# Merge weights finished in one step, four merge operations moved ahead, and the low weight parts last in each product

## The chip, the cores and the metric

The kernel runs on one core of a Trainium2 chip. The core has a matrix engine (TensorE, PE in the profile, with weight loads listed as PEld), a vector engine (DVE), a scalar engine (ACT), GpSimd (POOL), and a queue (SP) from which this kernel issues all of its transfers between HBM and the core's own memory (SBUF). Matrix products land in the accumulators (PSUM). The metric is the device time of one execution in microseconds; less is better.

## The reference

Two layers over a sequence of 1024 rows of 1024 values. Layer 0 is dilated sliding-window attention, gated; layer 1 is a state-space layer. The change lies in layer 0:

```python
proj = h @ w_in
qkv = proj[..., :n_qkv].reshape(B, S, 3, N_GROUPS_A, ATTN_HEADS, HEAD_DIM)
z = proj[..., n_qkv:]
outs, lses = [], []
for g, (window, dilation) in enumerate(DILATED_GROUPS):          # three groups
    o, l = dilated_group_attention(qkv[:, :, 0, g], qkv[:, :, 1, g], qkv[:, :, 2, g],
                                   rel_bias, window, dilation)
    outs.append(o)
    lses.append(l)
wts = jax.nn.softmax(jnp.stack(lses), axis=0)
o = jnp.sum(wts[..., None] * jnp.stack(outs).astype(jnp.float32), axis=0)
o = o.reshape(B, S, ATTN_WIDTH).astype(h.dtype)
return (o * jax.nn.silu(z)) @ w_out
```

So for each of 16 heads three attention outputs are computed, one for each group, and merged with weights that are a softmax over the three groups' log-sum-exps. The kernel calls these the merge's weights (the "group weights").

## The kernel before

The kernel first norms and transposes the input and computes all values v (up to about 334 us), then runs the attention (about 334 to 1050 us), then the gate, the output projection and layer 1. The attention works on *units*: unit m is the pair of heads p = m // 3 in group g = m mod 3, 24 units in all (class `Unit`).

Numbers are held in two parts. `split` (L100) makes a high part on ACT (L104) and a low part, the source minus the high part, on DVE or POOL (L105); a product then takes three matmuls instead of one: high x high, high x low, low x high.

The projection to queries and keys of one unit is done with seven products in place of eight (a Strassen scheme). `product(i)` (L560) accumulates twelve matmuls of 128 x 128 weights on 512 columns into bank X (i = 0, 5, 6, 3) or Y (i = 1, 4, 2); its operand is `w[:, y, ...]`, y = 0 the high and y = 1 the low part of the weights. `weights(i)` (L544) makes these two parts, the high one on ACT, the low one on POOL (tile wqk), and four such tiles exist at a time. `sums` and `qk` move the banks on and make q and k, with their low parts ql and kl on POOL (L105). `load` (L537) brings a unit's raw weights, two tiles of 512 KB (wraw), each as soon as the tile of the unit before is no longer read.

The rest of a unit's attention is spread over the two units that follow: `logits` (PE L665, DVE L671), `exps` (ACT L687), `T` (transposes on PE, L693, tile pt), `split_weights` (ACT and DVE, tile ph), `PV` (PE L742), `store` (ACT L761 and DVE L762). In the loop over m, `cur` is the unit whose projection runs, `one` the unit before, `two` the one before that, `nxt` the next one.

When the third group of a pair is done, its three outputs are merged, during the next two units. `put_ms` writes maxima and sums to HBM and `merge_load` reads them compactly; `merge_maxima` follows at the end of that unit. In the next unit, the one whose `two` has g = 0 and which is called a merging unit here, `merge_weights` (L810 to L813, four small operations on POOL) and `merge_store` (a reciprocal on DVE, L821, a multiplication on POOL, L822, and a write to HBM, wt_dr, L824) finish the weights. `merge` (L935) is a generator: each step of it issues one POOL operation. In the merging unit there are six: two multiplications of group 2's output by its weights and two of group 0's (L946), each with two loads of 128 KB (mw<-wt_dr, L945), and two additions (L949). Four buffers (ring tag b) hold the loaded weights. `more(n)` takes n steps of it. In other units `more` takes steps of `rotations` or of the merge's second part.

The order is written out by hand: `Program` (`step`, `run`) keeps the instructions of each step in this order on PE, ACT, DVE and POOL. SP's queue isn't bound by it; the planner that builds the program orders transfers by what is ready in its own simulated time and by priority, and the loads of raw weights have a raised priority. Each engine's queue, SP's too, is then worked off strictly in order on the chip.

Of the kernel before, what the change touches and what calls it, by code (L numbers as in the profile page):

```python
# [316 lines left out]
class Quads:  # L317
# [48 lines left out]
    done, jobs = 0, {}  # L366

    def quad(self, raw, order, product, banks, use):


# [144 lines left out]
class Unit:  # L515
# [44 lines left out]
    def product(self, i):  # L560
        c = self.c
        if i == 0:
            self.X = c.psx.tile([P, H], F32, tag="x", name="x")
        elif i in (1, 4):
            self.Y = c.psy.tile([P, H], F32, tag="y", name="y")
        ps = self.X if i in (0, 5, 6, 3) else self.Y
        w, rows = self.w.pop(i), c.forms[i]
        order = [(b, x, y) for b in range(4) for x, y in ((0, 0), (1, 0), (0, 1))]
        for m, (b, x, y) in enumerate(order):
            c.nc.tensor.matmul(ps, w[:, y, b * P:b * P + P], rows[x][:, b, :], start=i in (0, 1, 4) and m == 0,  # L570
                               stop=m == len(order) - 1, skip_group_check=True)
# [215 lines left out]
def merge_load(c, p):  # L787
    cm, e, d = c.compact
    src = bass.AP(c.ms_dr.tensor, c.ms_dr.offset + p * 3 * 4096, [[32, 64], [2048, 6], [1, 32]])
    c.nc.sync.dma_start(cm.rearrange("p g m n -> p (g m) n"), src)  # L790
# [66 lines left out]
def attn_units(c, w_in):  # L857

    nc, tc = c.nc, c.tc
    units = [Unit(c, m) for m in range(24)]  # L860
    c.outputs = [[] for _ in range(8)]
    step = Program(c)

    units[0].load(w_in)
    for i in (0, 1, 5):
        if i == 5:
            units[0].difference()
        units[0].weights(i)
    for m in range(26):
        cur = units[m] if m < 24 else None  # L870
        one = units[m - 1] if 1 <= m < 25 else None
        two = units[m - 2] if m >= 2 else None
        nxt = units[m + 1] if m + 1 < 24 else None

        def run(*steps):
            for unit, name, *args in steps:
                if unit is not None:
                    step(getattr(unit, name), *args)

        if one and one.g == 0:  # L880
            extra = rotations(c, one.p)
        elif two and c.merge is not None:
            extra = merge(c, c.merge, c.outputs[c.merge], two.g)
            if two.g == 1:
                c.merge = None
        else:
            extra = iter(())

        def more(n):
            for _ in range(n):  # L890
                step(next, extra, None)

        weigh = c.merge if two and two.g == 0 else None
        run((cur, "product", 0), (cur, "sums", 0), (two, "PV", 0, 1), (two, "T", 1, 0),
            (two, "split_weights", 1, 0), (two, "exps", 1, 1), (two, "store", 0, 1))
        if weigh is not None:
            step(merge_weights, c)
        run((cur, "weights", 6), (cur, "weights", 4))
        if weigh is None:
            more(1)  # L900
        run((cur, "product", 1), (cur, "sums", 1), (one, "logits", 0),
            (two, "PV", 1, 0), (two, "T", 1, 1), (two, "split_weights", 1, 1), (two, "store", 1, 0), (cur, "weights", 3))
        if weigh is not None:
            step(merge_store, c, weigh)
        else:
            more(2)
        run((cur, "product", 5), (cur, "sums", 5), (one, "logits", 1), (two, "PV", 1, 1))
        if two:
            c.pair = two.p
            step(put_ms, c, two.g, two.ms)  # L910
            if two.g == 2:
                merge_load(c, two.p)
        run((one, "split_v", 0), (one, "load_v", 1), (two, "store", 1, 1), (one, "exps", 0, 0), (cur, "weights", 2),
            (nxt, "load", w_in))
        more(5 if weigh is None else 2)
        run((cur, "product", 6), (cur, "sums", 6), (one, "logits", 2), (one, "exps", 0, 1), (cur, "product", 4),
            (cur, "sums", 4), (one, "T", 0, 0), (one, "split_weights", 0, 0), (one, "split_v", 1), (cur, "load_v", 0),
            (one, "logits", 3), (nxt, "difference"), (nxt, "weights", 0))
        if weigh is not None:
            more(4)  # L920
        run((cur, "qk", 1), (cur, "qk", 4),
            (cur, "product", 3), (cur, "qk", 3), (nxt, "weights", 1), (one, "PV", 0, 0), (one, "T", 0, 1),
            (one, "split_weights", 0, 1), (one, "exps", 1, 0), (cur, "product", 2), (cur, "sums", 2),
            (cur, "qk", 2), (one, "store", 0, 0))
        if two and two.g == 2 and two.p < 7:
            step(merge_maxima, c)
        run((nxt, "weights", 5))
        more(9)
        if two and two.g == 2:
            if two.p < 7:  # L930
                c.merge = two.p
            else:
                c.last = c.outputs[7]

def merge(c, p, O, part):  # L935


    nc = c.nc
    halves = [slice(n * H, n * H + H) for n in range(2)]
    for g in ((2, 0), (1,))[part]:  # L940
        for n, cols in enumerate(halves):
            w = c.slot("mw", tag="b")
            off = c.wt_dr.offset + (p * 3 + g) * 2048 + n * H
            for h in range(2):
                nc.sync.dma_start(w[HEADS[h]], bass.AP(c.wt_dr.tensor, off + h * S, [[0, 64], [1, H]]))  # L945
            nc.gpsimd.tensor_tensor(O[g][:, cols], O[g][:, cols], w, op=ALU.mult)  # L946
            yield
    for cols in halves:
        nc.gpsimd.tensor_tensor(O[2][:, cols], O[2][:, cols], O[part][:, cols], op=ALU.add)  # L949
        yield  # L950
    if part == 0:
        return
    if p >= EARLY:
        for cols in halves:
            w = c.slot("mg", tag="b")
            nc.sync.dma_start(w, c.g_dr[p, :, cols])
            nc.gpsimd.tensor_tensor(O[2][:, cols], O[2][:, cols], w, op=ALU.mult)
            yield
    nc.sync.dma_start(c.on_dr[p], O[2])
# [19 lines left out]
def attention(c, a):  # L979
# [60 lines left out]
    c.psa, c.psx, c.psy = c.ps("psa", 1), c.ps("psx", 1), c.ps("psy", 1)  # L1040
    c.attn = c.es_attn.enter_context(tc.tile_pool(name="attn", bufs=1, side="right", reuse_waits="tile"))
    attn_units(c, a["w_in"])
    return h

# [542 lines left out]
def rotations(c, et):  # L1587


    nc = c.nc  # L1590
    v = nc.gpsimd
    t = c.attn.tile([P, 192], F32, tag="rotc", name="rotc", bufs=1)
    for at, off, w in ((0, 0, 16), (128, S, 8)):
        src = bass.AP(c.tab_dr.tensor, c.tab_dr.offset + off + et * 4 * w, [[S + H, P], [32 * w, 2], [1, 4 * w]])
        nc.sync.dma_start(t[:, at:at + 8 * w].rearrange("p (n x) -> p n x", n=2), src)
    rot2 = [[t[:, at + n * 4 * w:at + (n + 1) * 4 * w].rearrange("p (k x) -> p k x", k=4) for n in range(2)]
            for at, w in ((0, 16), (128, 8))]
    shape = [P, 4, 8, 16]
    xr, xi = (y.unsqueeze(2).to_broadcast(shape) for y in rot2[0])
    wr, wi = (y.unsqueeze(3).to_broadcast(shape) for y in rot2[1])  # L1600

    def store(n, t):
        for s in range(2):
            dst = bass.AP(c.rot_dr.tensor, c.rot_dr.offset + (et * 3 + n) * 64 * S + s * P, [[S, 64], [256, 4], [1, P]])
            nc.sync.dma_start(dst, t[HEADS[s]].rearrange("p (k x) -> p k x", k=4))

    for part in range(2):
        out, tmp = c.slot("rt", tag="b"), c.slot("rtmp", tag="b")
        o, t = (x.rearrange("p (k j x) -> p k j x", k=4, j=8) for x in (out, tmp))
        v.tensor_tensor(o, xr, wi if part else wr, op=ALU.mult)  # L1610
        yield
        v.tensor_tensor(t, xi, wr if part else wi, op=ALU.mult)
        yield
        v.tensor_tensor(o, o, t, op=ALU.add if part else ALU.subtract)
        store(part, out)
        yield
    yield
    yield
    nc.scalar.activation(tmp, out, AF.Copy, scale=-1.0)
    store(2, tmp)  # L1620
# [381 lines left out]
```

## Time and profile before

| what | value |
|---|---|
| runs before | 1621.3, 1616.12, 1618.36 us; median 1618.36 |
| the profiled execution's own time | 1613.09 us |
| its span | 1610.9 us |
| PE, DVE, ACT, POOL busy | 98%, 65%, 50%, 43% of the span |
| granted TensorE clock | 0.997 |

The span is the time from the first to the last instruction in the profiled execution. Times in the profile's timeline are counted from its start. A timeline row gives the start, the duration, the engine, the line, the operation, the tile written and the tiles read, and the count of instructions in the row; in brackets stands the engine's idle time before it and what ended it.

### The profile page before, as it was taken

The page shows a single profiled execution, that of the slowest core. Times are in us where ns is not written, and L with a number is a line of the kernel's source. Part 1 is how long each engine was busy: PE and PEld are TensorE (multiplying, and loading weights), DVE is VectorE, ACT ScalarE, POOL GpSimd, SP SyncE. Part 2 cuts the span into 40 slices and gives each one's busy share as a digit, 9 for nine tenths or more (in the row PEclk, how much of TensorE's full clock was granted, in tenths as well). Part 3 has the DMA queues.
Part 4 walks back from the last instruction along what each step waited for, and adds up shares of the span by engine and source line. Part 5 has one row for each costly group of instructions (what it writes and reads, how often), then busy time and mean ns, then how long its engine had stood idle before and what let it go on. Part 6 is the DMA issues. An engine that isn't in the chain of part 4 may idle for free.

```text
span 1610.9 us, 26891 instructions
## 1 busy us (share of the span) xinstructions
PE 1578.2 (98%) x9462; PEld 1339.7 (83%) x9462; DVE 1053.9 (65%) x2532; ACT 806.2 (50%) x2004; POOL 699.0 (43%) x586
## 2 busy tenths in 40 slices
PE   8999999999999999999999999999999999999998
PEld 6889999988887888888888878887888888878886
DVE  8798889945555655655555656658563999855533
ACT  5232223337777677767677677754453223433411
POOL 1000001026577677686777777535220455522121
PEclk9999999999999999999999999999999999999999
DMA  6323444433223333414324333548347888565432
GB/s 257 118 54 111 155 145 147 150 116 89 70 70 106 101 90 102 111 60 110 103 70 125 95 103 101 129 146 234 104 157 204 247 246 258 171 190 175 157 118 79
DMA packets 185808, 216.43 MB, mean 134 GB/s; under 512 B 43060, under 2 KB 139079, under 8 KB 185161
## 3 DMA queue, kind: packets, MB, share of 16 engines
q1 hardware_dynamic: 185672, 214.72, 45.0%
q8 instruction: 74, 1.21, 0.3%
q14 instruction: 62, 0.50, 0.1%
HBM read 155.61 MB, written 59.06 MB: 133 GB/s over the span
## 4 chain that ended last, share of the span: by engine, by line
PE 61%; DVE 7%; POOL 6%; DMA 5%; issue 2%; SPq 2%; ACT 1%; DVEq 0%; POOLq 0%; ACTq 0%
PE x L570 14%; PE y L570 10%; PE pso L1178 10%; PE psj L130 8%; PE pso L742 5%; PE psq L449 4%; PE psl L665 4%; PE pt L693 3%; DMA mw<-wt_dr 2%; DVE T L1702 2%; PE psb L130 1%; DVE T L1707 1%; POOL O L946 1%; POOL O L949 1%; POOL wqk L105 1%
## 5 line engine op out<-in xcount | busy, mean ns | idle before, releaser
L105 POOL TENSOR_TENSOR wqk<-wraw,wqk 128x512 fp32r<-128x512 f32 x161 | 210.5, 1316 | 125.9 <-ACT wqk L104 119.1
L687 ACT ACTIVATE lg<-lg,nm 128x128 f32<-128x128 f32 (+1 forms) x384 | 168.6, 443 | 1.6
L105 DVE TENSOR_TENSOR ph<-pt,ph 128x512 fp32r<-128x512 f32 (+2 forms) x160 | 93.9, 620 | 99.0 <-ACT ph L104 98.9
L570 PE MATMUL x<-v,wqk 128*128 128x512 f32 x576 | 146.4, 403 | 0.7 <-ACT u L583 0.7
L570 PE MATMUL y<-v,wqk 128*128 128x512 f32 x576 | 145.4, 401 | 0.0
L671 DVE CUSTOM_DVE_ANT_0 lg<-psl,T 128x128 f32<-128x128 f32 (+1 forms) x384 | 110.6, 347 | 42.7 <-PE psl L665 41.6
L570 PE MATMUL x<-hh,wqk 128*128 128x512 f32 x384 | 130.4, 400 | 0.0
L1554 POOL TENSOR_TENSOR Ks<-Ks,O 128x16 f32<-128x16 f32 x8 | 4.1, 513 | 290.3 <-ACT Ks L1552 276.3
L570 PEld LDWEIGHTS y<-v,wqk 128*128 128x128 f32 x576 | 105.5, 188 | 23.7
L104 ACT CAST wqk<-wraw 128x512 fp32r<-128x512 f32 x168 | 102.5, 617 | 42.4 <-DVE wraw L550 24.5
L570 PEld LDWEIGHTS x<-v,wqk 128*128 128x128 f32 x576 | 104.5, 189 | 22.6 <-ACT u L583 1.1
L449 PE MATMUL psq<-whi,v 128*128 128x256 f32 x640 | 119.7, 284 | 0.0
L742 PEld LDWEIGHTS pso<-ph,vs 128*128 128x128 f32 x736 | 97.4, 189 | 9.8 <-DVE ph L105 0.8
L130 PE MATMUL psj<-h1h,whi 128*128 128x512 f32 (+1 forms) x272 | 103.4, 385 | 1.1 <-ACT h1h L104 1.1
L742 PE MATMUL pso<-ph,vs 128*128 128x256 f32 (+1 forms) x736 | 103.4, 281 | 0.2
L104 ACT CAST ph<-pt 128x512 fp32r<-128x512 f32 (+2 forms) x160 | 78.6, 533 | 48.1 <-PE pt L693 47.8
L130 PE MATMUL psj<-h1l,whi 128*128 128x512 f32 (+1 forms) x272 | 101.8, 379 | 0.2 <-DVE h1l L105 0.2
L449 PEld LDWEIGHTS psq<-whi,v 128*128 128x128 f32 x640 | 99.8, 189 | 1.2 <-ACT whi L104 0.6
L1205 POOL TENSOR_TENSOR xr<-xr,y 128x512 f32<-128x512 f32 x30 | 38.2, 1295 | 128.2 <-DVE y L1204 90.5
L104 ACT CAST whi<-v 128x1024 fp32r<-128x1024 f32 x35 | 36.7, 1050 | 108.4 <-PE psq L449 93.7
L449 PE MATMUL psq<-wlo,v 128*128 128x256 f32 x320 | 90.2, 283 | 0.0
L570 PEld LDWEIGHTS x<-hh,wqk 128*128 128x128 f32 x384 | 72.2, 188 | 17.6
(310 smaller groups left out, 4378.2 us busy)
## 6 DMA issues: line engine op xcount, KB each, us to landing
wraw<-in_w_in_dram SPq DMA_DIRECT2D x56, 512.0 KB
v<-in_w_v_dram SPq DMA_DIRECT2D x24, 512.0 KB
mw<-wt_dr SPq DMA_DIRECT2D x84, 128.0 KB
vp<-v_dr SPq DMA_DIRECT2D x32, 256.0 KB
wraw<-in_ssm_w_in_dram SPq DMA_DIRECT2D x16, 512.0 KB
v_dr<-v SPq DMA_DIRECT2D x30, 256.0 KB
ca_dr<-ca SPq DMA_DIRECT2D x32, 144.0 KB
CA<-ca_dr SPq DMA_DIRECT2D x8, 576.0 KB
```

The lines of the kernel that those rows point to most:

```text
L104: c.last_hi = nc.scalar.copy(hi, src).ins
L105: return (engine or nc.vector).tensor_tensor(lo, src, f32(hi), op=ALU.subtract)
L130: nc.tensor.matmul(ps, w[n == 2][:, k * P:k * P + P], h[n == 1][:, k, :], start=first and k == 0 and m == 0, stop=m == len(order) - 1 and ...
L449: nc.tensor.matmul(o, r[x][:, k, ts], w[y][:, k, :], skip_group_check=True, start=i in (0, 4, 5) and t % 2 == k == n == 0, stop=k == 3 and ...
L570: c.nc.tensor.matmul(ps, w[:, y, b * P:b * P + P], rows[x][:, b, :], start=i in (0, 1, 4) and m == 0, stop=m == len(order) - 1, skip_group ...
L665: nc.tensor.matmul(psl[:, h, o], x[HEADS[h], qs], y[HEADS[h], ks], start=j == js[0] and i == 0, stop=i == 2, skip_group_check=True)
L671: nc.vector.tensor_tensor_reduce(self.lg[u, j][:, h], psl[:, h, o], self.bt[:, h, 256 - w:256], scale=1.0, scalar=-3.0e38, op0=ALU.add, op ...
L687: c.nc.scalar.activation(t, t, AF.Exp, bias=self.nm[:, h, b:b + 1], accum_out=ms[:, col:col + 1])
L693: c.nc.tensor.transpose(pt[:, n * P:(n + 1) * P], self.lg[u, j][:, h, part * P:part * P + P], c.ident)
L742: nc.tensor.matmul(o, l, r, start=n == 0, stop=n == len(jobs) - 1, skip_group_check=True)
L1178: nc.tensor.matmul(ps, x[:, k, ts], y[:, k, cols], start=n == m == 0, stop=n == KT - 1 and m == len(todo) - 1)
L1205: nc.gpsimd.tensor_tensor(x[:, ns], x[:, ns], y, op=ALU.add)
```

## The change

In every product the eight matmuls with the high part of the weights are issued first, the four with the low part last; before, each block of four had its own three in a row. In a merging unit `merge_weights` and `merge_store` are done together behind `split_weights(1, 0)` and ahead of `exps(1, 1)` and `store(0, 1)` of `two`; before, `merge_weights` came behind these two and `merge_store` behind `weights(3)`. The first four of the merge's six operations (all of L946) come ahead of `weights(0)` of `nxt`, the two additions behind it; before, two came ahead and four behind. In every unit `weights(2)` comes ahead of `exps(0, 0)` of `one`. No operation is added or removed.

```diff
-        order = [(b, x, y) for b in range(4) for x, y in ((0, 0), (1, 0), (0, 1))]
+        order = [(b, x, 0) for b in range(4) for x in range(2)] + [(b, 0, 1) for b in range(4)]
...
         run((cur, "product", 0), (cur, "sums", 0), (two, "PV", 0, 1), (two, "T", 1, 0),
-            (two, "split_weights", 1, 0), (two, "exps", 1, 1), (two, "store", 0, 1))
+            (two, "split_weights", 1, 0))
         if weigh is not None:
             step(merge_weights, c)
-        run((cur, "weights", 6), (cur, "weights", 4))
+            step(merge_store, c, weigh)
+        run((two, "exps", 1, 1), (two, "store", 0, 1), (cur, "weights", 6), (cur, "weights", 4))
         if weigh is None:
             more(1)
...
-        if weigh is not None:
-            step(merge_store, c, weigh)
-        else:
+        if weigh is None:
             more(2)
...
-        run((one, "split_v", 0), (one, "load_v", 1), (two, "store", 1, 1), (one, "exps", 0, 0), (cur, "weights", 2),
+        run((one, "split_v", 0), (one, "load_v", 1), (two, "store", 1, 1), (cur, "weights", 2), (one, "exps", 0, 0),
             (nxt, "load", w_in))
-        more(5 if weigh is None else 2)
+        more(5 if weigh is None else 4)
         run((cur, "product", 6), (cur, "sums", 6), (one, "logits", 2), (one, "exps", 0, 1), (cur, "product", 4),
             (cur, "sums", 4), (one, "T", 0, 0), (one, "split_weights", 0, 0), (one, "split_v", 1), (cur, "load_v", 0),
             (one, "logits", 3), (nxt, "difference"), (nxt, "weights", 0))
         if weigh is not None:
-            more(4)
+            more(2)
```

## The prediction

> **What bounds the kernel now.** I read the page's totals first, then TensorE's waits, then each engine's timeline over one stretch in which it waits. In the totals, PE is busy in 98% of the span.
>
> ```profile
> span 1610.9 us, 26891 instructions
> PE 1578.2 (98%) x9462; PEld 1339.7 (83%) x9462; DVE 1053.9 (65%) x2532; ACT 806.2 (50%) x2004; POOL 699.0 (43%) x586
> ```
>
> So a change can only pay where PE waits. The list of waits, PE alone, has one entry that the diff touches:
>
> ```profile
> PE y L570 <- POOL wqk L105: 8.7, 6, 1.9
> ```
>
> Six times a product (L570) waits for the low part of its weights, made on POOL (L105): 8.7 us, 1.45 us each. Six is the number of units that merge a pair (pairs 0 to 6, one unit each) and still have a unit after them. I take the first, where the merging unit ends with the product at 498.04 and the next begins at 500.92. PE's timeline:
>
> ```profile
> 483.57 0.39 PE L665 MATMUL psl<-kl,qh 64*128 64x256 f32 x2
> ...
> 492.10 0.82 PE L693 MATMUL pt<-identr,lg 128*128 128x128 f32 x6
> ...
> 498.04 3.04 PE L570 MATMUL y<-v,wqk 128*128 128x512 f32 x12
> 500.92 0.39 PE L570 MATMUL x<-hh,wqk 128*128 128x512 f32 x1
> ...
> 503.69 1.03 PE L742 MATMUL pso<-ph,vs 128*128 128x256 f32 x8
> ...
> 505.16 0.48 PE L570 MATMUL y<-hh,wqk 128*128 128x512 f32 x1
> 505.47 0.40 PE L570 MATMUL y<-hl,wqk 128*128 128x512 f32 x1
> 507.36 0.73 PE L570 MATMUL y<-hh,wqk 128*128 128x512 f32 x2 [1.49 <-POOL wqk L105]
> ...
> 510.67 0.73 PE L693 MATMUL pt<-identr,lg 128*128 128x128 f32 x5
> ```
>
> A row ends where its last matmul is modelled to end, so the pitch comes from the row of twelve: (3.04 - 0.39) / 11 = 0.24, say 0.235 us. Product 1 of the next unit issues two matmuls (505.16, 505.47); the third, the first with low weights, starts at 507.36 instead of about 505.70. Lost: 1.66 us. That is 0.17 more than the idle of 1.49, because the modelled end (0.40) runs past the pitch. Over all six: 8.7 + 6 x 0.17 = **9.7 us**. This is everything the edited loop can win from PE's waits.
>
> Why POOL is late there:
>
> ```profile
> 479.58 0.23 POOL L813 TENSOR_TENSOR cm<-cm 64x32 f32<-64x32 f32 x1
> 480.52 3.80 POOL L105 TENSOR_TENSOR wqk<-wraw,wqk 128x512 fp32r<-128x512 f32 x3 [0.70 <-PE pt L693]
> 484.46 0.39 POOL L822 TENSOR_TENSOR cm<-cm,cm 64x96 f32<-64x96 f32 x1
> 489.81 1.30 POOL L105 TENSOR_TENSOR wqk<-wraw,wqk 128x512 fp32r<-128x512 f32 x1 [4.97 <-ACT wqk L104]
> 492.58 2.61 POOL L946 TENSOR_TENSOR O<-O,mw 128x512 f32<-128x512 f32 x2 [1.47 <-DMA mw<-wt_dr]
> 495.14 1.75 POOL L105 TENSOR_TENSOR wqk<-wraw,wqk 128x512 fp32r<-128x512 f32 x1
> 497.94 2.56 POOL L946 TENSOR_TENSOR O<-O,mw 128x512 f32<-128x512 f32 x2 [1.05 <-DMA mw<-wt_dr]
> 500.45 2.55 POOL L949 TENSOR_TENSOR O<-O,O 128x512 f32<-128x512 f32 x2
> 502.95 1.30 POOL L105 TENSOR_TENSOR ql<-p,qh 128x512 fp32r<-128x512 f32 x1
> 504.20 1.88 POOL L105 TENSOR_TENSOR kl<-u,kh 128x512 fp32r<-128x512 f32 x1
> 506.05 1.26 POOL L105 TENSOR_TENSOR wqk<-wraw,wqk 128x512 fp32r<-128x512 f32 x1
> ```
>
> POOL idles 4.97, 1.47 and 1.05 us, the last two for the weights' loads (mw), and from 497.94 on runs without a break to 507.32, when the low part is done. The date that decides is the landing of the second group's loads, 497.9. SP's queue and the chain of waits show where that comes from:
>
> ```profile
> 484.34 0.35 SPq L537 DMA_DIRECT2D wraw<-in_w_in_dram  x1
> 484.87 0.59 SPq L824 DMA_DIRECT2D wt_dr<-cm  x1
> ...
> 487.42 1.52 SPq L624 DMA_DIRECT2D vp<-v_dr  x2
> 489.05 2.41 SPq L945 DMA_DIRECT2D mw<-wt_dr  x4
> 491.56 0.53 SPq L537 DMA_DIRECT2D wraw<-in_w_in_dram  x1
> 492.19 3.01 SPq L945 DMA_DIRECT2D mw<-wt_dr  x5
> ```
>
> ```profile
> 492.68 5.12 DMA mw<-wt_dr
> ```
>
> wt_dr is written right after L822, and the eight loads of its two groups follow at 489.05 and 492.19, the second four behind the 512 KB load of wraw. SP isn't ordered by the program's steps: the fifth load of the last row already belongs to the next unit. It goes by what is ready.
>
> **The change, part by part.** *Low parts last* (L568). The twelve matmuls stay the same, at the same pitch; the low weights are needed at the ninth instead of the third, 6 x 0.235 = 1.41 us later. By itself it cuts the stall of 1.66 to 0.25, and the six to about 1.5 us: worth 8.2. In the other products nothing waits, so it is worth nothing there.
>
> *Merge weights and store ahead of exps and store(0,1)*, in merging units only. The four small operations keep their place on POOL, since nothing of POOL's stood between. L822 moves from 484.46 to right behind the reciprocal, so wt_dr is written before the three wqk of 480.52 instead of after them: at about 480.8, 4.1 us earlier. POOL stood idle for ACT until 480.52, so L822 (0.39, from about 480.3) delays the three by some 0.15 us. That is hidden by the idle 4.97 behind them. On DVE the reciprocal becomes a wait:
>
> ```profile
> 479.83 0.69 DVE L762 TENSOR_TENSOR O<-O,pso 64x512 f32<-64x512 f32 x1 [1.69 <-ACT O L761]
> ...
> 482.25 0.08 DVE L671 DVE_READ_ACCUMULATOR2_ANT ms<- 128x1 f32 x1
> ...
> 484.04 0.34 DVE L821 RECIPROCAL cm<-cm 64x32 f32<-64x32 f32 x1
> ...
> 494.30 1.43 DVE L105 TENSOR_TENSOR vs<-vp,vs 128x512 fp32r<-128x512 f32 x1
> ```
>
> It waits for L813 (ends 479.81). Behind it stand L762, sums(1) and the reductions up to 482.33, which free the bank for PE's logits at 483.57. They slip by 0.36 us out of 1.24 us of room, and from 484.04 on DVE is where it was. Cost 0; with that room gone, 6 x 0.36 = 2.2 us.
>
> *weights(2) ahead of exps(0,0)*, in all 24 units:
>
> ```profile
> 487.12 0.21 ACT L682 ACTIVATE nm<-ms 128x8 f32<-128x8 f32 x1
> ...
> 489.04 0.19 ACT L687 ACTIVATION_READ_ACCUMULATOR lg<-lg,nm 128x1 f32 x1
> 489.13 0.60 ACT L104 CAST wqk<-wraw 128x512 fp32r<-128x512 f32 x1
> ...
> 494.01 0.63 ACT L104 CAST wqk<-wraw 128x512 fp32r<-128x512 f32 x1
> ...
> 508.39 0.20 ACT L687 ACTIVATION_READ_ACCUMULATOR lg<-lg,nm 128x1 f32 x1
> ```
>
> The cast goes from 489.13 to 487.12, the exponentials 0.60 later, ending 489.8, while PE's transposes need them at 492.10: hidden by PE's own products. POOL's low part then runs 487.7 to 489.0 instead of 489.81, which also frees wraw two microseconds earlier, so the load of 491.56 can go at about 489.5.
>
> *Four merge operations ahead of weights(0), two adds behind.* On POOL the order becomes L946 x4, wqk(0), L949 x2, ql, kl, wqk(1). From the landing T of the second group to the end of wqk(1) there now lie 9.38 (497.94 to 507.32) plus the wqk(0) that moved in, 1.25: 10.63 us. PE wants it at the ninth matmul, 505.16 + 8 x 0.235 = 507.04. So the stall is gone if T is at most 496.4; for wqk(0) itself, wanted at 500.92 + 1.88 = 502.8, T may be 498.9. T is now 497.9. The trace doesn't show the moved loads. Bounds: at best they go out as soon as wt_dr has landed (between 0.6 us after its issue and 489.05 - 484.87 = 4.2 us), so the second group lands about 4 us earlier, 494; at worst SP keeps its order, they follow vp at 489.05 as now, and T is unchanged. I take the first, nearer to the row with the fifth mw, which shows SP issuing what is ready: at 481 the load of 484.34 isn't, since it waits for the third wqk (480.52 + 3.80 = 484.32), and vp comes three microseconds after that. With T about 494, wqk(1) is done at about 504.6, 2.4 us ahead of PE.
>
> **Contention on POOL.** The wqk at 495.14 took 1.75 us and the one at 489.81 1.30; the slow one overlaps the 1.43 us subtraction of 494.30 on DVE. After the change more of POOL's work lies beside DVE's. At worst all seven operations between T and wqk(1)'s end that don't show it yet are slowed by 0.45, 3.2 us, 0.8 more than the 2.4 to spare: 6 x 0.8 = 4.8 us come back. At best none. I take none, since DVE has few subtractions of two SBUF tiles there. The Trainium skill (GPSIMD Engine Reference, 8. Key points) says that GpSimd shares its SBUF interfaces with VectorE and contends with instructions that have two SBUF inputs; by that rule alone the sum would lean to the 4.8, and the row of 495.14 agrees with it.
>
> **Sum.** 1613.09 is the profiled execution's own time, 2.2 above its span and 5.3 below the median of the runs shown. 1613.09 - 9.7 + 0.4 for a little that may be late next = 1603.8, which is 1618.36 - 9.3 = **1609.0** on the median. What is late next is in the unit behind: transposes at 510.67 come 1.66 us earlier, 509.0, and need exponentials that end at 508.59.
>
> **Rivals.**
> *T doesn't move* (SP keeps mw behind vp). Then wqk(1) ends at 497.94 + 10.63 = 508.57, PE stalls 1.53 instead of 1.66, as the later need is eaten by wqk(0) moving behind the merge. Gain 6 x 0.13 = 0.8: 1617.6. For it: vp and ms_dr hold SP until 488.9. Against it: the order by readiness.
> *The next unit takes half.* The transposes of 510.67, or casts ahead of them, come 0.8 us late: 0.8 x 6 = 4.8 given back, 1613.5. For: 0.4 us of room only. Against: ACT's and DVE's chain there starts behind L949, which is then earlier.
> *The mw loads get ahead of the weights' load.* Eight loads at 0.60 (2.41 / 4) hold SP for 4.8 us and put 1 MB ahead of the 512 KB of 484.34, which ACT's cast at 494.01 needs, with everything on ACT behind it.
>
> ```profile
> 484.00:500.00 16.00, 16.00 (x108) 13.38 (x105) 10.65 (x36) 12.37 (x39) 8.35 (x8) 1.00 0.74 190
> ```
>
> At this stretch's 190 GB/s it lands at 484.9 + 1.5 MB / 190 = 493, in time. At half that rate, 501.5: seven ACT operations of about 0.6, from that cast to the ph cast, end at 505.7, DVE's part at 506.4, and PV of 503.69 starts 2.7 late. Against 1.66 now that is 6 x 1.0 = 6 us worse: 1624.4. It decides from a landing of about 500.5 on.
>
> **How the numbers follow.** A measurement of this kernel tells about 0.3% (4.9 us) from no change. Forecast 0.67, T unmoved 0.18, half taken 0.09, slower 0.06. The forecast's own range is 1605 to 1613 (gain 9.7 or less what contention brings back, and some 2 us of scatter as in the runs shown); half taken straddles the limit, T unmoved lies within it. Faster 0.67 + half of 0.09, less a little scatter: 0.69; same 0.24; slower 0.07. Range for 8 in 10: 1604.5 to 1617.
>
> **What would show it.** Right: no wait of PE on POOL wqk in the list; SP's first mw ahead of vp, at 481 to 485 us in that unit; L946 x4 in one run ending before 496; L822 before the three wqk. Wrong: L946's second pair still at 497 to 498, PE's wait still 1.5 us but at the ninth matmul; or new waits of PE on ACT or DVE in the unit behind, or the 512 KB load landing after 494.

## The result and the profile after

The changed kernel takes 1610.29 us in the median of five runs (1605.64 to 1611.7), beside 1617.08 us for the kernel before. The ratio is 0.9945, 95% interval 0.9925 to 0.9966: 8.9 us faster, between 5.5 and 12. (It is the ratio of the means; the two medians lie 6.8 us apart.) The forecast was 9.3 us and 1609.0.

The page's first lines after, and in the list of PE's waits the entries that matter (total, times, longest):

```profile
span 1608.8 us, 26878 instructions
```

```profile
PE pso L1177 <- DVE hl L105: 2.5, 1, 2.5
...
PE psj L130 <- DMA hl<-a_dr: 2.0, 1, 2.0
...
PE psj L130 <- DMA hh<-a_dr: 1.0, 1, 1.0
...
PE y L570 <- POOL wqk L105: 0.4, 1, 0.4
```

The wait on POOL wqk was 8.7 us at six places and is 0.4 at one. Two new entries stand ahead of it: PE waits 3.0 us in all for hh and hl<-a_dr, which the list before doesn't have. (Lines behind L903 carry a number one lower than before; L945 is the old L946.)

How long the attention stage takes can be read from the products: the view of line L570 gives each group's first and last start. Before, first products with hh and last with v:

```profile
L570 PE MATMUL x<-hh,wqk x384: 388/392/505, 334.4 to 1039.5; 128*128 128x512 f32 x192
...
L570 PE MATMUL y<-v,wqk x576: 390/393/500, 346.5 to 1043.8; 128*128 128x512 f32 x192
```

After:

```profile
L570 PE MATMUL x<-hh,wqk x384: 388/393/505, 333.6 to 1029.6; 128*128 128x512 f32 x192
...
L570 PE MATMUL y<-v,wqk x576: 390/393/500, 345.7 to 1033.9; 128*128 128x512 f32 x192
```

709.4 us became 700.3: 9.1 of the 9.7 us. A whole product of twelve matmuls takes 3.04 us in both kernels (the row of 498.04 before, that of 497.22 below), so the new order inside a product costs PE nothing.

POOL in the first merging unit, after. The unit begins 0.8 us earlier than before:

```profile
479.45 0.38 POOL L822 TENSOR_TENSOR cm<-cm,cm 64x96 f32<-64x96 f32 x1 [0.46 <-DVE cm L821]
479.80 3.79 POOL L105 TENSOR_TENSOR wqk<-wraw,wqk 128x512 fp32r<-128x512 f32 x3
487.00 1.28 POOL L105 TENSOR_TENSOR wqk<-wraw,wqk 128x512 fp32r<-128x512 f32 x1 [3.42 <-ACT wqk L104]
488.24 3.91 POOL L945 TENSOR_TENSOR O<-O,mw 128x512 f32<-128x512 f32 x3
495.14 1.47 POOL L945 TENSOR_TENSOR O<-O,mw 128x512 f32<-128x512 f32 x1 [2.98 <-DMA mw<-wt_dr]
496.56 1.76 POOL L105 TENSOR_TENSOR wqk<-wraw,wqk 128x512 fp32r<-128x512 f32 x1
...
503.28 1.74 POOL L105 TENSOR_TENSOR wqk<-wraw,wqk 128x512 fp32r<-128x512 f32 x1
```

SP's queue there:

```profile
479.86 0.59 SPq L824 DMA_DIRECT2D wt_dr<-cm  x1
481.82 2.41 SPq L944 DMA_DIRECT2D mw<-wt_dr  x4
484.33 0.53 SPq L537 DMA_DIRECT2D wraw<-in_w_in_dram  x1
484.96 1.08 SPq L944 DMA_DIRECT2D mw<-wt_dr  x2
...
489.42 0.46 SPq L537 DMA_DIRECT2D wraw<-in_w_in_dram  x1
...
490.75 3.65 SPq L944 DMA_DIRECT2D mw<-wt_dr  x6
```

And PE, at the end of the unit and at product 1 of the next:

```profile
497.22 3.04 PE L570 MATMUL y<-v,wqk 128*128 128x512 f32 x12
...
504.34 0.48 PE L570 MATMUL y<-hh,wqk 128*128 128x512 f32 x1
...
506.29 1.08 PE L570 MATMUL y<-hh,wqk 128*128 128x512 f32 x4
...
508.07 0.73 PE L693 MATMUL pt<-identr,lg 128*128 128x128 f32 x5
```

wt_dr is written at 479.86 instead of 484.87, and the first six loads follow from 481.82 on, four and then two. Three of the four multiplications run in one piece behind the wqk of weights(2). The fourth waits 2.98 us: its two loads come at 490.75, behind ms_dr, vp and a load of wraw. The low part of weights(1) is done at 503.28 + 1.74 = 505.02, and PE takes it without a wait at 506.29, 1.95 us after the product's first matmul.

### The profile page after: what moved, and what is told of

Its sections match the earlier page's. It is cut to its first block, busy times and chain, and to the rows that moved or that the text cites. A ratio compares the mean times of both kernels' runs of the same rounds, so it can differ in the third digit from the quotient of the medians.

```text
span 1608.8 us, 26878 instructions
## 1 busy us (share of the span) xinstructions
PE 1578.9 (98%) x9462; PEld 1340.9 (83%) x9462; DVE 1054.1 (66%) x2532; ACT 805.2 (50%) x2004; POOL 702.5 (44%) x586
## 4 chain that ended last, share of the span: by engine, by line
PE 63%; DVE 8%; DMA 6%; POOL 3%; issue 2%; SPq 2%; ACT 1%; DVEq 0%; POOLq 0%; ACTq 0%
PE x L570 15%; PE y L570 12%; PE pso L1177 10%; PE psj L130 6%; PE pso L742 5%; PE psl L665 4%; PE psq L449 4%; PE pt L693 3%; DVE T L1701 2%; PE psb L130 1%; DMA taps<-k_dr 1%; DVE T L1706 1%; DMA wfr<-in_ssm_w_out_dram 1%; POOL Y L1725 1%; DMA wraw<-in_w_in_dram 1%
## 5 line engine op out<-in xcount | busy, mean ns | idle before, releaser
L570 PE MATMUL x<-v,wqk 128*128 128x512 f32 x576 | 146.4, 403 | 0.7 <-ACT u L583 0.7
L570 PE MATMUL y<-v,wqk 128*128 128x512 f32 x576 | 145.4, 401 | 0.0
L570 PE MATMUL x<-hh,wqk 128*128 128x512 f32 x384 | 130.5, 400 | 0.0
L570 PEld LDWEIGHTS y<-v,wqk 128*128 128x128 f32 x576 | 105.5, 188 | 23.7
L570 PEld LDWEIGHTS x<-v,wqk 128*128 128x128 f32 x576 | 104.5, 189 | 22.6 <-ACT u L583 1.1
L570 PEld LDWEIGHTS x<-hh,wqk 128*128 128x128 f32 x384 | 72.2, 188 | 18.0 <-DVE ql L108 0.4
```

## The experiments

All ratios are against the kernel before. Each of the three groups of runs had its own chip and its own runs of before beside it, so ratios within a group compare best. "The stage" is the attention stage, read as above from the first and the last of the two groups of matmuls.

**Each means alone.** First group.

```diff
 # on the kernel before
-        order = [(b, x, y) for b in range(4) for x, y in ((0, 0), (1, 0), (0, 1))]
+        order = [(b, x, 0) for b in range(4) for x in range(2)] + [(b, 0, 1) for b in range(4)]
```

> The kernel before with only the new order inside a product (low parts last). Theory A (each of the two means takes most of the stall by itself): POOL keeps its dates, so wqk(1) ends as before, 0.0 to 0.7 us behind the ninth matmul; PE's waits on POOL wqk fall from 8.7 to about 1.5 us, the attention stage from 709.4 to about 701.2 us, and since SP's order at the end of the attention is that of the kernel before, the handover to the gate costs nothing: 8 us faster than before in all, as much as the changed kernel or a little more. Rival B (the early merge does the work, the order in a product nothing): waits stay at 8.7, no change. Rival C (PE's pitch suffers from the new order): the twelve matmuls take over 2.85 us a product, 168 products, slower.

Measured: 0.9938 (0.9926 to 0.9951), 10.0 us. Its waits:

```profile
PE y L570 <- POOL wqk L105: 0.5, 1, 0.5
```

One line brings the whole gain. The stage takes 700.8 us, 8.6 less. 1.5 us of the stall had been expected to stay, and the list has 0.5; but it counts only idle time behind a matmul's modelled end. By the starts, where a product that doesn't stall begins its ninth matmul 1.95 us after its first, the six places lose 0.15, 0.14, 0.68, 0.13, 0.05 and 0 us: 1.15 in all.

```diff
 # on the changed kernel
-        order = [(b, x, 0) for b in range(4) for x in range(2)] + [(b, 0, 1) for b in range(4)]
+        order = [(b, x, y) for b in range(4) for x, y in ((0, 0), (1, 0), (0, 1))]
```

> The changed kernel with the old order inside a product. In the changed kernel wqk(1) of the first merging unit ends at 505.02, and PE begins product 1 at 504.34, so its third matmul would come at 504.8. Theory A: PE waits about 0.2 to 0.7 us at each of the six places, 1.5 to 4 us in all against 8.7 before, and the attention stage takes 702 to 704 us. The handover keeps the changed kernel's loss (PE waits for hh and hl<-a_dr, 3 us), so the whole is 2 to 5 us faster than before. Rival B (the early merge alone suffices): no wait on wqk, attention stage at 700.3. Rival D (only the order in a product counts): waits stay near 8.7.

Measured: 0.9950 (0.9937 to 0.9964), 8.1 us, more than the 2 to 5 expected; the stage takes 702.0 us. Its waits:

```profile
PE y L570 <- POOL wqk L105: 2.0, 3, 1.4
```

So moving the merge nearly suffices too. The two means cover the same stall, and their gains don't add.

**The merge's store put back.** First group.

```diff
 # on the changed kernel
             step(merge_weights, c)
-            step(merge_store, c, weigh)
...
-        if weigh is None:
+        if weigh is not None:
+            step(merge_store, c, weigh)
+        else:
             more(2)
```

> The changed kernel with the merge's store (reciprocal, multiplication, write of wt_dr) back behind weights(3), the four merge operations still ahead of weights(0). Theory A: the second group's loads land as late as before or about 1 us earlier, POOL has 10.6 us of work from there, so PE waits 0.5 to 1.5 us at the ninth matmul in each of six units: 3 to 9 us of the 9.7 are back, and the kernel is 0 to 5 us faster than before. Rival B (the order in a product alone is enough cover): waits under 1.5 us in all, as fast as the changed kernel.

Measured: 0.9976 (0.9964 to 0.9988), 3.9 us. Its waits, POOL and PE in the same place:

```profile
PE y L570 <- POOL wqk L105: 8.2, 6, 2.2
```

```profile
494.71 6.04 POOL L946 TENSOR_TENSOR O<-O,mw 128x512 f32<-128x512 f32 x4 [5.44 <-DMA mw<-wt_dr]
...
507.56 1.26 POOL L105 TENSOR_TENSOR wqk<-wraw,wqk 128x512 fp32r<-128x512 f32 x1
```

```profile
508.87 1.20 PE L570 MATMUL y<-hh,wqk 128*128 128x512 f32 x4 [1.43 <-POOL wqk L105]
```

The stall is back, at the ninth matmul now (the last four of the product). POOL waits for the first pair of loads until 494.71, and the four multiplications end at 500.75. In the kernel with the order alone they end at 500.11, which is only 0.2 us sooner once the 0.42 us are taken off by which product 1 starts later here. But there weights(0) is made before the last two of them; here it is queued behind all four, 1.25 us, with the adds, ql, kl and weights(1) behind it, and the low parts last don't cover that. So with the store late, four ahead does harm.

The waits are a little shorter than before (8.2 against 8.7), yet the stage takes 710.7 us, 1.3 more. The granted TensorE clock accounts for that. Behind the longest of the six waits, 2.17 us, it is 0.79 over 8 us, which is 8 x 0.21 = 1.7 us; behind the longest of the kernel before, 1.92 us, it stays at 1.00:

```profile
689.00:697.00 8.00, 6.53 (x29) 5.72 (x30) 2.41 (x4) 4.52 (x14) 7.84 (x8) 0.79 0.01 2
```

```profile
958.00:966.00 8.00, 6.08 (x34) 5.24 (x34) 2.41 (x4) 4.97 (x15) 7.84 (x7) 1.00 0.01 2
```

(Each line: the stretch; busy time of PE, PEld, DVE, ACT, POOL with their instructions; granted clock; DMA share; GB/s.) So the 3.9 us by which this kernel measured faster don't come from its stage. Outside the stage its span has 903.8 us, between the 901.5 and 906.7 of two profiles of the kernel before; where the 3.9 us come from stays open.

**What weights(2) ahead of exps(0,0) does.** Second group.

> The changed kernel again, unaltered, on the chip and beside the runs of before that the next kernels use, so that they can be set against it. Expected: 0.9945 of before as in its first measurement, the attention stage at 700 us, the handover 4 us longer than before with PE's waits on the reload of hh and hl<-a_dr.

Measured: 0.9913 (0.9890 to 0.9936), 1605.86 us; no wait on wqk in the list. So the same kernel, 8.9 us faster the first time, is 14.1 us faster here, which wasn't expected. In the profiles its stage is 699.0 us instead of 700.3; of the 8.0 us between the two spans, 6.5 lie behind the stage's last product.

```diff
 # on the changed kernel
-        run((one, "split_v", 0), (one, "load_v", 1), (two, "store", 1, 1), (cur, "weights", 2), (one, "exps", 0, 0),
+        run((one, "split_v", 0), (one, "load_v", 1), (two, "store", 1, 1), (one, "exps", 0, 0), (cur, "weights", 2),
```

> The changed kernel with weights(2) back behind exps(0,0) in every unit. Theory A (this step only frees raw weights sooner, and the two other steps have cover to spare): POOL's first multiplication of the merge comes 2 us later, behind the low part of weights(2) at 489.8, wqk(1) ends 0 to 1.5 us later than 505.0 against a need at 506.2, PE's waits on wqk stay under 2 us in all, no change beyond 0.15% against the changed kernel. Rival G (the step is needed: the wraw load released late holds SP's queue, and the last loads of merge weights stand behind it): waits of 3 us or more come back, 0.2% or more slower than the changed kernel.

Measured: 0.9906 (0.9884 to 0.9928), the stage 699.0 us, no wait on wqk either. The step isn't needed. SP's queue in this kernel, in the first merging unit and at the end of the attention:

```profile
490.67 2.12 SPq L944 DMA_DIRECT2D mw<-wt_dr  x2
492.88 0.53 SPq L537 DMA_DIRECT2D wraw<-in_w_in_dram  x1
...
1032.13 0.42 SPq L1106 DMA_DIRECT2D hh<-a_dr  x1
...
1037.72 0.58 SPq L1131 DMA_DIRECT2D fz<-on_dr  x1
```

Here the last pair of merge loads goes ahead of the 512 KB of wraw; the fourth multiplication waited 0.46 us instead of 2.98. At the end the reload (hh<-a_dr) goes out ahead of the load of fz, which the last part of this section is about.

```diff
 # on the kernel before: the new order in a product, and
-        ... (two, "store", 1, 1), (one, "exps", 0, 0), (cur, "weights", 2),
+        ... (two, "store", 1, 1), (cur, "weights", 2), (one, "exps", 0, 0),
```

> The kernel before with the new order inside a product and weights(2) ahead of exps(0,0), the merge where it was. Theory A: as the kernel with the new order alone, 0.9938 of before, attention stage 700 to 701 us, since nothing waits for what this step brings forward. Rival H (the earlier release of wraw lets the 512 KB load get ahead of the loads of merge weights, which then land later): POOL's second pair of multiplications starts later than 497.4 in the first merging unit and waits of PE on wqk come back, 1 to 4 us.

Measured: 0.9977 (0.9961 to 0.9993), where the order in a product alone had 0.9938. Its waits, SP and POOL:

```profile
PE y L570 <- POOL wqk L105: 7.2, 6, 1.4
```

```profile
489.25 0.41 SPq L537 DMA_DIRECT2D wraw<-in_w_in_dram  x1
489.76 6.88 SPq L945 DMA_DIRECT2D mw<-wt_dr  x9
```

```profile
494.38 3.50 POOL L946 TENSOR_TENSOR O<-O,mw 128x512 f32<-128x512 f32 x2 [5.47 <-DMA mw<-wt_dr]
```

For comparison, the kernel with the order alone:

```profile
489.23 2.41 SPq L945 DMA_DIRECT2D mw<-wt_dr  x4
491.74 0.53 SPq L537 DMA_DIRECT2D wraw<-in_w_in_dram  x1
```

```profile
492.79 1.29 POOL L946 TENSOR_TENSOR O<-O,mw 128x512 f32<-128x512 f32 x1 [1.93 <-DMA mw<-wt_dr]
```

Rival H holds, and by more than the 1 to 4 us it was given: weights(2) done early frees wraw early, its 512 KB load then gets ahead of all merge loads, the first multiplication starts 1.6 us later, and the waits go from 0.5 to 7.2 us (the stage from 700.8 to 707.9). In the changed kernel the same step brings no wait back: there six of the eight merge loads are out before that load of wraw.

> The kernel before, unaltered, for a second profile: its first profiled execution, 1613.09 us, lies 5 us below the median of its runs. Theory J: the attention stage takes 709.4 us as in the first profile, and the 4 to 7 us that are missing lie outside it, in the first 40 us and in layer 1, where the granted clock dips. Rival K: the attention stage itself varies by several us from run to run.

Measured: 0.9991 (0.9970 to 1.0013) against itself. This profile of the kernel before:

```profile
span 1616.8 us, 26891 instructions
```

```profile
L570 PE MATMUL x<-hh,wqk x384: 388/392/505, 335.2 to 1041.0; 128*128 128x512 f32 x192
...
L570 PE MATMUL y<-v,wqk x576: 390/393/500, 347.3 to 1045.3; 128*128 128x512 f32 x192
```

The attention stage takes 710.1 us, 0.7 more than in the first profile, of 5.9 us more in the span. So the scatter between these two executions lies mostly outside the stage that was changed.

**The end of the attention.** First group. In the changed kernel SP's queue there is:

```profile
1039.32 0.58 SPq L1131 DMA_DIRECT2D fz<-on_dr  x1
1040.01 0.59 SPq L1106 DMA_DIRECT2D hh<-a_dr  x1
1040.66 0.42 SPq L1106 DMA_DIRECT2D hl<-a_dr  x1
```

The reload of hh and hl, wanted by the products behind the attention, fills space that the last product reads; that one starts its last matmul at 1033.9. A load of fz (merged output, for the gate) stands ahead of it and waits 5.0 us for POOL's merge:

```profile
SPq L1131 <- POOL O L945: 5.0, 1, 5.0
```

The same stretch of work before, 10 us later by the clock, and after, where PE waits for the reload:

```profile
1054.00:1062.00 8.00, 8.00 (x43) 6.63 (x42) 6.01 (x22) 5.71 (x23) 6.96 (x5) 1.00 0.67 190
```

```profile
1044.00:1052.00 8.00, 4.97 (x19) 3.81 (x18) 3.39 (x19) 1.94 (x4) 3.00 (x3) 0.81 0.99 337
```

PE is idle for 3.0 us, and the granted clock over the 8 us is 0.81: 8 x 0.19 = 1.5 us more. Together 4.5 us, half of the 9.1 that the stage gave back in that execution. The Trainium skill (TensorE: Matmul & The Clock Gate, Part 1: The HAM clock gate) puts TensorE at half its clock after at least one idle window of about 3.4 us. The half agrees: the matmuls from 1050.82 to 1052.10 start 0.43 us apart, those from 1052.46 on 0.23. The length doesn't: the longest unbroken idle time here is 2.0 us.

```diff
 # on the changed kernel
+        reload = nc.sync.dma_start(f32(a21[n]), ...).ins
...
+        with c.tc.issue_after(reload):
             nc.sync.dma_start(f, c.on_dr[p]...)          # both loads of fz
```

> The changed kernel, with the loads of fz ordered behind the reload of hh and hl<-a_dr on SP. Theory E (the handover's loss is SP's order: the reload, possible from about 1034.3 when the last product has read the space it fills, stands behind an fz load that waits for POOL until 1039.3): the reload is issued by about 1035, lands by 1044, PE's waits on a_dr (3.0 us) and the dip of the clock behind them go, and the kernel is 3 to 5 us faster than the changed one, 12 us faster than before. Rival F (the reload is slow for lack of DMA throughput, its issue doesn't matter): the waits stay, no change against the changed kernel.

Measured: 0.9922 (0.9910 to 0.9935), 12.6 us. SP's queue:

```profile
1034.85 0.33 SPq L1106 DMA_DIRECT2D hh<-a_dr  x1
```

The waits on a_dr are gone and the clock in that stretch is 1.00. Theory E holds for the mechanism. Its size isn't settled: the changed kernel has no run in this group, and in its second profile the same wait was 1.2 us, with no dip of the clock.

**Is four ahead needed?** Third group.

```diff
 # on the changed kernel: weights(2) back behind exps(0, 0), and
-        more(5 if weigh is None else 4)
+        more(5 if weigh is None else 2)
...
-            more(2)
+            more(4)
```

> The kernel before with the new order inside a product and the merge's weights finished early (store moved), but weights(2) behind exps(0,0) and two merge operations ahead of weights(0), four behind, as before. Theory A (the early store alone brings the merge weights in time; four ahead or two makes no difference to PE): no wait on wqk over 0.5 us in all, attention stage 699 to 701 us, as fast as the kernel without the weights(2) step. Rival L (four ahead is needed): wqk(1) ends late again, waits of 2 us or more.

Measured: 0.9910 (0.9886 to 0.9934), the stage 698.9 us, and no wait on wqk in the list. With the low parts last, the early store is enough; neither four ahead nor weights(2) is needed.

In the same group, the kernel without the weights(2) step and the one with the reload first were measured again:

> The changed kernel without the weights(2) step once more, beside the next one on one chip. Theory M: the reload of hh and hl<-a_dr goes out by 1033 as in its first run, PE doesn't wait at the handover, and the two agree within 0.15%: about 0.991 to 0.992 of before.

> The changed kernel with the reload put ahead of the fz loads once more, beside the one without the weights(2) step. Theory M: both have lost the handover's wait, so within 0.15% of each other. Rival N (the weights(2) step is of use once the handover is mended): this one is 0.15% or more faster.

Measured: 0.9919 (0.9895 to 0.9944) and 0.9915 (0.9888 to 0.9942), the stages 698.9 and 699.1 us; neither list has a wait on wqk or a_dr. The three kernels of this group can't be told apart, from each other or from the changed kernel's 0.9913 in the second group. None of them is shown to be better than the changed kernel. Their 13 to 15 us are more than the some 10.5 by which their stage is shorter than in the first profile of before; where the rest lies isn't located.

## Why the prediction was right, point by point

**What could be won.** Put at 9.7 us. The attention stage gave 9.1 us back between the first two profiles, and 10.2 to 10.5 in the six runs whose list has no wait on wqk. Right, a little low.

**Low parts last.** Put at 8.2 us by itself with 1.5 left. Alone it left 1.15 by the starts, and the stage was 8.6 us shorter. Right in mechanism and in size; the 10.0 us of the whole execution are 1.4 more than the stage shows.

**Store ahead.** wt_dr was put 4.1 us earlier and went 5.0 earlier by the clock, 4.2 of it against the unit's own start. On DVE the reciprocal does wait for POOL, and the copy behind it follows at once:

```profile
479.03 0.34 DVE L821 RECIPROCAL cm<-cm 64x32 f32<-64x32 f32 x1 [1.71 <-POOL cm L813]
479.40 0.69 DVE L762 TENSOR_TENSOR O<-O,pso 64x512 f32<-64x512 f32 x1
```

That is the 0.36 us slip that was called hidden; no wait of PE on DVE in the list comes from it.

**The landing T** (of the loads for the second pair). Put at 494, with wqk(1) done at 504.6 and 2.4 us to spare; it was 495.1, 505.0 and 506.29 - 505.02 = 1.3. On the clock of before, where everything lies 0.8 us later, T was about 496.0: 2 us late, and only 0.4 under the limit of 496.4. That limit counted two multiplications behind T. In fact only the fourth was left, so POOL had 9.88 us of work from T on instead of 10.63. The order by readiness was read rightly from the fifth mw row, but the second group wasn't loaded in one piece, and one of the prediction's signs of being right failed: four multiplications in one run ending before 496. Three came in one run; the fourth ended at 496.61.

The kernel with the store late comes nearest to the rival in which T stays. That rival's stall of 1.53 us a unit is 9.2 us in six; measured were 8.2 of idle time, which with 0.17 a place for the modelled end is 9.2 too. The path isn't the same: there POOL's long wait is for the first pair, and it doesn't wait for the second.

**weights(2), the step that was misjudged.** The prediction wrote that it "also frees wraw two microseconds earlier, so the load of 491.56 can go at about 489.5", and gave that no price. The rival on the other side, in which raw weights and merge loads get in each other's way, had the merge loads ahead and the raw weights late. It is the reverse: the raw load gets ahead and the merge loads come late. With the merge where it was, that is worth 6.7 us of waits (7.2 against 0.5). In the changed kernel it took 0.8 us of room: wqk(1) was done 1.3 us before PE wanted it, and 2.1 us before (505.22 against 507.29) in the kernel without the step.

**What was left out, and luck.** The sum ended at the last unit. Past it, the planner put a waiting load ahead of the reload, which cost 4.5 us in the first profile and is one reason why the two profiled executions lie only 2.1 us of span apart. The 0.4 us set aside for "a little that may be late next" was looked for in the next unit; there the transposes followed at 508.07 without a wait. That the first measurement came within 0.4 us of the 9.3 is partly luck: the same kernel measured 14.1 us faster the second time, most of the difference outside the stage. The mechanism, which the stage shows, doesn't rest on that.

**Contention.** It was put at none, since DVE was said to have few subtractions of two SBUF tiles there. Two of POOL's wqk took 1.76 and 1.74 us instead of 1.30, and each overlaps a DVE operation on two SBUF tiles (L542 at 496.47, L550 at 502.99). That is 0.9 us in this unit, which the room covered.

## What to carry to other kernels

When one consumer waits for the last-made part of its operand, first look whether it can use that part last: one line did here about what all the moved steps together did, and the gains of two covers over the same stall don't add. In an in-order transfer queue, releasing a buffer earlier isn't free: it also moves that buffer's load ahead of others, so ask of every earlier release which transfer it now overtakes. And follow a reordering to the end of the stage, where the planner may place a load that waits ahead of one that doesn't.

## What the runs showed of the hardware

In these traces a longer wait of TensorE can cost more than itself, in one step. A wait of 3.0 us, broken by one matmul, cost 1.5 us more through the granted clock (0.81 over 8 us), and the single one of 2.17 us in the kernel with the store late 1.7 us more (0.79). One of 1.2 us, in the second profile of the changed kernel at the place of the 3.0, didn't touch the clock:

```profile
1043.00:1051.00 8.00, 6.81 (x34) 5.41 (x33) 3.76 (x19) 5.16 (x20) 1.59 (x1) 1.00 1.04 328
```

Nor did the 1.92 us of the kernel before, and nor did a wait of 2.5 us later in the changed kernel's first profile (pso <- DVE hl, ended at 1108.26; granted clock 1.00 from 1106 to 1114). So the price isn't proportional to the length, and between 2.17 and 2.5 us the length alone doesn't decide; what does isn't shown.
